# Later weight sums and an exchanged product in the up projection of a decoder trunk's MLP

## The chip, the cores and the metric

The kernel runs on one core of a Trainium2 chip. The metric is device time in microseconds (us) of one execution. TensorE (PE) multiplies, VectorE (DVE) and ScalarE (ACT) do elementwise work, GpSimd (POOL) is nearly unused in the part that changes, and SyncE (SP) issues most DMAs.

## The reference

A trunk of two layers works on x of 1024 x 1024 float32. Each layer is attention and then an MLP with a squared ReLU; the change touches the MLP alone.

```
def squared_relu_mlp(h, w_up, w_down):
    a = jax.nn.relu(h @ w_up)
    return (a * a) @ w_down

# in each layer i:
x = x + squared_relu_mlp(rmsnorm(x, mlp_norm_g[i]), mlp_w_up[i], mlp_w_down[i])
```

h is 1024 x 1024, w_up 1024 x 4096, w_down 4096 x 1024.

## The kernel before

**Products.** Both MLP matmuls are done by Strassen's scheme with seven products in place of eight (numbered 1 to 7, Winograd's form). Each product is itself done in three passes, since every operand is split into a high part (a copy in a rounded format, made by ACT, L99) and a low part (source less high part, made by DVE, L100): high by high, high by low, low by high, in lines L1700 to L1702.

**Up units.** `mlp` runs over 16 units (`NP`), each 256 columns of `w_up`. A unit has seven products of 12 matmuls of 128x512. Its weights come as two halves of 512 KB (`load_raw`, L1619), into two tiles `mr` for even units and two tiles `d` for odd ones. `gain_w` multiplies them by the norm's gain, eight ACT instructions (L1592). `sum_w` forms four weight sums on DVE (L1635 to L1638). `prep_w` splits one operand of a product (L99, L100) into one of seven pairs of tiles that go round; the loop asks for it three products ahead.

**Banks.** Products 1, 6, 7 and 4 of a unit add up in one PSUM bank (`psu`), 2 in a second, 5 and 3 in a third (`psv`). After 1, 6 and 5 ACT copies the bank out (L1743). After 2, 7 and 3 DVE adds bank and copy (L1756) and squares (L1735). After 4 ACT takes the ReLU (L1747) and DVE multiplies (L1748). So with the order 1, 2, 6, 5, 7, 3, 4 there is always a product in another bank between two that share one. Results go to DRAM (`hd`, L1738).

**Down.** `Down` reads them back and multiplies with `w_down`. Its `begin` is called after each product of the last unit: after product 6 it takes the tile `f0`, which held the X operand of product 6 (`mqf` in the trace), and issues four loads of `w_down` into it (`load_b`, L1859); after product 5 the same with `f1`. The first down steps split these loads and the results of the up units, and multiply into `psy` (L2053 to L2055).

**Order.** The code records instructions; a planner lays out each engine's queue from that. It starts what its own reckoning of time has ready and prefers what was recorded earlier among that. Each engine then runs its queue in that order. For units 0 and 1, whose products go 1, 2 early and then 6, 6, 5, 5, 7, 7, 3, 3, 4, 4, the order is written out by hand; `tc.issue_after` holds some of that work behind a given instruction.

Of the kernel before, what the change touches and what calls it, by code (L numbers as in the profile page):

```python
# [55 lines left out]
def trunk(  # L56
# [39 lines left out]
    def split(src, hi, lo, scale=None):  # L96

        if scale is None:
            r = nc.scalar.activation(hi, src, AF.Copy)  # L99
            return r, nc.vector.tensor_tensor(lo, src, f32(hi), ALU.subtract)  # L100
        else:
            nc.scalar.activation(hi, src, AF.Copy, scale=scale)
            nc.vector.scalar_tensor_tensor(lo, src, scale, f32(hi), ALU.mult, ALU.subtract)
# [845 lines left out]
    def units_of(h):  # L949
        return units if h < H - 1 else units_end  # L950
# [153 lines left out]
    seq = [(h, u) for h in range(H) for u in units_of(h)]  # L1104
# [78 lines left out]
    NP = FF // 256  # L1183
    TORD = list(range(NT))
    SUB = ALU.subtract

    def k4(ap):
        return ap.rearrange("p (k c) -> p k c", k=4)
# [419 lines left out]
    def mlp(layer, m, early_w=None, early_mm=None):  # L1608

        X, xr = m.X, m.xr  # L1610
        V, G = nc.vector, nc.vector.tensor_tensor
# [3 lines left out]
        def load_raw(i):  # L1615
            r = [m.raw() for _ in range(2)] if i % 2 == 0 else [m.t(f"d{j}") for j in range(2)]
            raws[i] = r = [t_.rearrange("p a (b c) -> p (a b) c", c=256) for t_ in r]
            for h in range(2):
                nc.sync.dma_start(out=r[h], in_=wsrc[:, 4 * h : 4 * h + 4, 256 * i : 256 * i + 256])  # L1619

        ss = []

        def gain_w(i):
            for h in range(2):
                scale_w(layer, raws[i][h], 4 * h)

        def sum_w(i):
            if i < 2:
                ss.append([m.t(f"i{j}")[:, 0, :] for j in (1, 3, 5)] if i == 0 else [*[m.t("d2")] * 2, m.t("i7")[:, 0, :]])
                if i == 1:  # L1630
                    ss[1][0:2] = [ss[1][0][:, j, :] for j in range(2)]
            r = raws.pop(i)
            a11, a12, a21, a22 = r[0][:, :, 0:P], r[1][:, :, 0:P], r[0][:, :, P:256], r[1][:, :, P:256]
            s1, s2, s4 = [k4(a) for a in ss[i % 2]]
            G(s1, a21, a22, ALU.add)  # L1635
            G(s2, s1, a11, SUB)
            G(a21, a11, a21, SUB)
            G(s4, a12, s2, SUB)  # L1638
            sums[i] = {1: a11, 2: a12, 3: s4, 4: a22, 5: s1, 6: s2, 7: a21}

        def pair(t_):
# [21 lines left out]
        def prep_w(i, p):  # L1663
            a = sums[i][p]
            n = hct[0]
            hct[0] += 1
            if n < 7:
                hl.append([k4(v) for v in opens[n]()])
            hi, lo = hl[n % 7]
            split(a, hi, lo)  # L1670
            return hi, lo
# [6 lines left out]
        def prep_x(p, cols=range(4)):  # L1678
            for j in cols:
                c = slice(j * P, (j + 1) * P)  # L1680
                if layer and (p != 6 and j < 2 or len(cols) == 4):
                    if j % 2:
                        continue
                    c = slice(j * P, (j + 2) * P)
                src = m.t2[j] if p == 6 else xr[{5: 0, 7: 1, 4: 2, 3: 3}[p]][:, :, c]
                hi, lo = [v[:, :, c] for v in X[p]]
                split(src, hi, lo)
# [83 lines left out]
                write(7, i, h)  # L1771

        seq = [(i, p) for p in (6, 5, 7, 3, 4) for i in range(2)]
        seq += [(i, p) for i in range(2, NP) for p in (1, 2, 6, 5, 7, 3, 4)]
        LA = 4
        ready = {}

        def go(i, p, w):
            evac(i, p, up_mm(i, p, w))
# [12 lines left out]
        else:  # L1792
            gain_w(0)
        sum_w(0)
        prep_x(6, range(3))
        load_raw(1)
# [5 lines left out]
        with tc.issue_after(m.last_n.ins):  # L1802
            gain_w(1)
        sum_w(1)
        ready[(1, 6)] = prep_w(1, 6)
        prep_x(5, (3,))
        ready[(0, 5)] = prep_w(0, 5)
        X[7] = [m.t("g0", F32R), m.t("g1", F32R)]
        X[3] = [m.t("g2", F32R), m.t("g3", F32R)]
        with tc.issue_after(m.last_n.ins):  # L1810
# [8 lines left out]
        for n, (i, p) in enumerate(seq):  # L1819
            for q_ in seq[n : n + LA]:  # L1820
                if q_ not in ready:
                    ready[q_] = prep_w(*q_)
            if (i, p) == (1, 7):
                load_raw(2)
                gain_w(2)
                sum_w(2)
            if p == 4 and 0 < i < NP - 2:
                load_raw(i + 2)
            if p == 2 and i < NP - 1:
                gain_w(i + 1)  # L1830
            if p == 6 and 2 <= i < NP - 1:
                sum_w(i + 1)
            go(i, p, ready.pop((i, p)))
            if i == NP - 1:
                dn.begin(p)
# [341 lines left out]

    jw, early = {}, []
    mlp(0, m0, lambda: jw.update(early_w()), early_mm)
    m0.rp.release()  # L2180
    kv1p = pool("kv1p")
# [183 lines left out]
    m1 = Mlp(1, x1)  # L2365
    wo_strassen(1, wq, [f0, f1], m1)
    mlp(1, m1)
    m1.rp.release()
    m1.s.release()
# [35 lines left out]
```

## Time and profile before

| what | value |
|---|---|
| median of 3 runs | 2110.15 us (2108.54 to 2110.25) |
| the profiled execution | 2112.17 us |
| its span, first to last instruction | 2110.5 us |
| PE busy | 2071.6 us (98%), 9880 matmuls |
| DVE, ACT busy | 1493.9 us (71%), 1142.9 us (54%) |
| up units of layer 0 and of layer 1 in the trace | about 541 to 854 and 1477 to 1797 us |

The profiled execution is one run of its own, 2.0 us above the median; 1.7 us of it lie outside the span. Matmuls are pipelined: one of 128x512 is shown with 0.39 us, and the next starts after about 0.23 us. A wait of PE is therefore seen best in the distance between two starts.

### The profile page before, as it was taken

To read this page: it belongs to the slowest core of one execution; us is meant where nothing else is said; L and a number is where in the kernel's file an instruction comes from. 1 tells how busy PE (TensorE), PEld (TensorE's weight loads), DVE (VectorE), ACT (ScalarE), POOL (GpSimd) and SP (SyncE) were. 2 spreads that over 40 slices of the span, in tenths; PEclk is the share of its full clock that TensorE was granted. 3 is DMA by queue.
4 is the path that set the end of the run, shared out by engine and by line. 5 is a ranking of instruction groups with operands and counts; after the bars stand their busy time and mean duration, and the time that the engine had idled before them with its cause. 6 is when DMAs were issued, how large, how long until landed. Compare 5 with 4: busy or idle time off the path is not lost.

```text
span 2110.5 us, 29217 instructions
## 1 busy us (share of the span) xinstructions
PE 2071.6 (98%) x9880; PEld 1699.8 (81%) x9880; DVE 1493.9 (71%) x2876; ACT 1142.9 (54%) x2461; POOL 204.7 (10%) x288
## 2 busy tenths in 40 slices
PE   7999999999999999999999999999999999999998
PEld 6988778778778888788888878778788887888887
DVE  7555688865977766797667543897976775976565
ACT  5445477776744453444445553877845443444452
POOL 0013100000000000031111231631000000000000
PEclk9999999999999999999999999999999999999999
DMA  7202123343254445976653211146344446844332
GB/s 247 68 1 76 46 63 90 105 146 100 96 184 146 139 154 195 325 254 205 212 165 95 75 31 30 41 156 234 122 152 146 165 140 225 316 152 154 117 119 90
DMA packets 181632, 294.47 MB, mean 140 GB/s; under 512 B 18557, under 2 KB 74346, under 8 KB 181482
## 3 DMA queue, kind: packets, MB, share of 16 engines
q1 hardware_dynamic: 171008, 264.25, 38.9%
q0 software_dynamic: 8048, 25.70, 3.5%
q10 hardware_dynamic: 2426, 2.65, 0.4%
q8 instruction: 78, 1.28, 0.2%
q14 instruction: 72, 0.59, 0.1%
HBM read 194.81 MB, written 85.25 MB: 133 GB/s over the span
## 4 chain that ended last, share of the span: by engine, by line
PE 76%; DVE 8%; DMA 8%; ACT 5%; issue 2%; SPq 0%; POOL 0%; DVEq 0%; ACTq 0%; POOLq 0%
PE psy L2053 5%; PE psy L2055 5%; PE psy L2054 5%; PE psz L2054 4%; PE psz L2053 4%; PE psz L2055 4%; PE pss L964 4%; PE pso L1006 3%; PE psu L1700 3%; PE psu L1702 3%; PE psu L1701 3%; DMA mr<-in_mlp_w_up_dram 3%; DMA d<-in_mlp_w_up_dram 3%; PE psf L108 2%; PE psf L110 2%; PE psf L109 2%
## 5 line engine op out<-in xcount | busy, mean ns | idle before, releaser
L1592 ACT ACTIVATE mr<-mr,gcol 128x256 f32<-128x256 f32 (+1 forms) x160 | 67.7, 479 | 79.0 <-DMA mr<-in_mlp_w_up_dram 64.4
L2053 PE MATMUL psy<-g 128*128 128x512 f32 x256 | 99.9, 390 | 0.0
L2054 PE MATMUL psy<-g 128*128 128x512 f32 x256 | 99.6, 389 | 0.0
L2055 PE MATMUL psy<-g 128*128 128x512 f32 x256 | 99.3, 389 | 0.0
L1592 ACT ACTIVATE d<-d,gcol 128x256 f32<-128x256 f32 x128 | 57.3, 499 | 75.5 <-DMA d<-in_mlp_w_up_dram 65.4
L99 ACT ACTIVATE g<-i 128x512 fp32r<-128x512 f32 x79 | 49.6, 628 | 88.3 <-PE psz L2054 41.2
L99 ACT ACTIVATE i<-mr 128x512 fp32r<-128x512 f32 x86 | 54.0, 628 | 68.6 <-PE psz L2054 20.0
L985 ACT ACTIVATE p<-pss 128x512 f32<-128x512 f32 x108 | 63.6, 593 | 41.1 <-PE pss L964 41.0
L100 DVE TENSOR_TENSOR g<-i,g 128x512 fp32r<-128x512 f32 x79 | 55.6, 704 | 40.7 <-ACT g L99 40.6
L99 ACT ACTIVATE uh<-i 128x512 fp32r<-128x512 f32 x66 | 41.6, 630 | 76.9 <-PE psy L2054 35.7
L100 DVE TENSOR_TENSOR pl<-p,ph 128x512 fp32r<-128x512 f32 (+1 forms) x96 | 61.6, 651 | 27.6 <-ACT ph L99 27.1
L839 DVE TENSOR_REDUCE m<-psx 128x1 f32<-128x128 f32 (+5 forms) x96 | 70.2, 748 | 11.0 <-PE psx L835 10.8
L2053 PE MATMUL psz<-g 128*128 128x512 f32 x192 | 74.7, 389 | 0.0
L2054 PE MATMUL psz<-g 128*128 128x512 f32 x192 | 74.7, 389 | 0.0
L2055 PE MATMUL psz<-g 128*128 128x512 f32 x192 | 74.7, 389 | 0.0
L100 DVE TENSOR_TENSOR uh<-i,uh 128x512 fp32r<-128x512 f32 x66 | 45.5, 689 | 36.7 <-ACT uh L99 36.7
L100 DVE TENSOR_TENSOR i<-mr,i 128x512 fp32r<-128x512 f32 x78 | 53.6, 687 | 21.2 <-ACT i L99 21.0
L99 ACT ACTIVATE ph<-p 128x512 fp32r<-128x512 f32 (+1 forms) x96 | 56.4, 599 | 1.3
L1928 DVE TENSOR_TENSOR mqf<-mqq,mqf 128x512 f32<-128x512 f32 x64 | 43.0, 687 | 19.3 <-DMA mqq<-in_mlp_w_down_dram 19.2
L2055 PEld LDWEIGHTS psy<-g 128*128 128x128 f32 x256 | 48.0, 188 | 10.0
L2053 PEld LDWEIGHTS psy<-g 128*128 128x128 f32 x256 | 48.1, 188 | 9.9
L2054 PEld LDWEIGHTS psy<-g 128*128 128x128 f32 x256 | 48.1, 188 | 9.8
(746 smaller groups left out, 6972.8 us busy)
## 6 DMA issues: line engine op xcount, KB each, us to landing
i<-hd SPq DMA_DIRECT2D x154, 256.0 KB
hd<-uh SPq DMA_DIRECT2D x76, 256.0 KB
hd<-ul SPq DMA_DIRECT2D x76, 256.0 KB
mr<-in_mlp_w_up_dram SPq DMA_DIRECT2D x36, 512.0 KB
hd<-x SPq DMA_DIRECT2D x72, 256.0 KB
mr<-hd SPq DMA_DIRECT2D x70, 256.0 KB
d<-in_mlp_w_up_dram SPq DMA_DIRECT2D x32, 512.0 KB
mqq<-in_mlp_w_down_dram SPq DMA_DIRECT2D x32, 512.0 KB
```

What stands on the lines that cost most here:

```text
L99: r = nc.scalar.activation(hi, src, AF.Copy)
L100: return r, nc.vector.tensor_tensor(lo, src, f32(hi), ALU.subtract)
L839: nc.vector.reduce_max(m8s[h][:, i : i + 1], ps[:, c], axis=AX, negate=True)
L964: return lambda: nc.tensor.matmul(o, a, b, skip_group_check=True, **kw)
L985: nc.scalar.activation(p, ps, AF.Exp, scale=SC)
L1006: mms.append(lambda: nc.tensor.matmul(o, a, b, skip_group_check=True, **kw))
L1592: nc.scalar.activation(w[:, k, :], w[:, k, :], AF.Copy, scale=g_mlp[layer][:, k0 + k : k0 + k + 1])
L1700: nc.tensor.matmul(ps, wh[:, k, :], xh[:, k, :], start=p in (1, 2, 5) and k == 0, stop=False, skip_group_check=True)
L1701: nc.tensor.matmul(ps, wh[:, k, :], xl[:, k, :], start=False, stop=False, skip_group_check=True)
L2053: nc.tensor.matmul(ps, ah[:, j, :], bh, start=p in (1, 5, 2) and k == 0, stop=False, skip_group_check=True)
L2054: nc.tensor.matmul(ps, ah[:, j, :], bl, start=False, stop=False, skip_group_check=True)
L2055: nc.tensor.matmul(ps, al[:, j, :], bh, start=False, stop=k == NP - 1, skip_group_check=True)
```

## The change

Three edits, in both layers. (1) Of the four sums of unit 0, the last two (`a21` and `s4`, L1637 and L1638) are recorded after the operand splits for (1, 6) and (0, 5) and the last columns of the X operands of 6 and 5. (2) In the last unit, product 6 comes second: 1, 6, 2, 5, 7, 3, 4. Operand splits and `begin(6)` follow that order. (3) For units 3 to 15, `gain_w` is recorded ahead of the previous unit's product 6 (before: of its product 2), and `sum_w` ahead of its product 5 (before: of its product 6).

```
-        ss = []
+        ss, held = [], []
...
             G(s1, a21, a22, ALU.add)
             G(s2, s1, a11, SUB)
-            G(a21, a11, a21, SUB)
-            G(s4, a12, s2, SUB)
+
+            def rest():
+                G(a21, a11, a21, SUB)
+                G(s4, a12, s2, SUB)
+
+            if i:
+                rest()
+            else:
+                held.append(rest)
...
-        seq += [(i, p) for i in range(2, NP) for p in (1, 2, 6, 5, 7, 3, 4)]
+        seq += [(i, p) for i in range(2, NP) for p in ((1, 2, 6, 5, 7, 3, 4) if i < NP - 1 else (1, 6, 2, 5, 7, 3, 4))]
...
         ready[(0, 5)] = prep_w(0, 5)
+        held[0]()
...
-            if p == 2 and i < NP - 1:
+            if p == 6 and 2 <= i < NP - 1:
                 gain_w(i + 1)
-            if p == 6 and 2 <= i < NP - 1:
+            if p == 5 and 2 <= i < NP - 1:
                 sum_w(i + 1)
```

## Rows read from the trace of the kernel before

**Rows 1.** The page: busy time and share of each engine.
```profile
PE 2071.6 (98%) x9880; PEld 1699.8 (81%) x9880; DVE 1493.9 (71%) x2876; ACT 1142.9 (54%) x2461; POOL 204.7 (10%) x288
```
**Rows 2.** Waits of PE: us in total, times, longest us.
```profile
PE psu L1700 <- ACT d L1743: 3.3, 7, 1.4
```
**Rows 3.** Timeline of PE, layer 0, end of up: start, us, instruction, [idle before].
```profile
850.82 0.39 PE L1702 MATMUL psv<-g,d 128*128 128x512 f32 x1
851.35 0.50 PE L1700 MATMUL psu<-x,d 128*128 128x512 f32 x1
851.70 0.40 PE L1701 MATMUL psu<-x,d 128*128 128x512 f32 x1
...
857.20 0.39 PE L2054 MATMUL psy<-g 128*128 128x512 f32 x1
858.57 0.50 PE L2053 MATMUL psy<-i,i 128*128 128x512 f32 x1 [0.99 <-DVE ul L1748]
```
**Rows 4.** Timeline of PE, layer 1, the same place.
```profile
1793.11 0.39 PE L1702 MATMUL psv<-g,d 128*128 128x512 f32 x1
1793.82 0.50 PE L1700 MATMUL psu<-x,d 128*128 128x512 f32 x1 [0.31 <-DVE x L1756]
...
1799.61 0.39 PE L2054 MATMUL psy<-g 128*128 128x512 f32 x1
1801.03 0.50 PE L2053 MATMUL psy<-i,i 128*128 128x512 f32 x1 [1.03 <-DVE ul L1748]
```
**Rows 5.** Timeline of DVE, layer 0, end of up.
```profile
850.00 0.69 DVE L100 TENSOR_TENSOR i<-mqf,i 128x512 fp32r<-128x512 f32 x1 [8.22 <-ACT i L99]
850.61 0.69 DVE L1756 TENSOR_TENSOR x<-psu,i 128x512 f32<-128x512 f32 x1
...
857.83 0.68 DVE L1748 TENSOR_TENSOR ul<-psu,ul 128x512 f32<-128x512 f32 x1
```
**Rows 6.** Timeline of ACT, layer 0, end of up.
```profile
837.96 0.58 ACT L1743 ACTIVATE d<-psu 128x512 f32<-128x512 f32 x1
...
849.34 0.63 ACT L99 ACTIVATE i<-mqf 128x512 fp32r<-128x512 f32 x1 [2.87 <-DMA mqf<-in_mlp_w_down_dram]
```
**Rows 7.** Timeline of SP's queue, layer 0, end of up.
```profile
843.08 5.82 SPq L1859 DMA_DIRECT2D mqf<-in_mlp_w_down_dram  x8
```
**Rows 8.** Timeline of PE, layer 0, products 1 and 2 of the last unit.
```profile
837.22 0.39 PE L1702 MATMUL psu<-mqq,i 128*128 128x512 f32 x1
837.45 0.39 PE L1700 MATMUL psv<-mqq,i 128*128 128x512 f32 x1
```
**Rows 9.** Timeline of ACT in a middle unit of layer 0.
```profile
708.63 0.91 ACT L1592 ACTIVATE mr<-mr,gcol 128x256 f32<-128x256 f32 x2 [3.09 <-DMA mr<-in_mlp_w_up_dram]
...
709.96 0.57 ACT L1743 ACTIVATE d<-psu 128x512 f32<-128x512 f32 x1
```
**Rows 10.** Timeline of PE, product 7 of the same unit.
```profile
710.59 0.50 PE L1700 MATMUL psu<-g,i 128*128 128x512 f32 x1
```
**Rows 11.** Timeline of DVE, layer 1, start of up.
```profile
1489.83 0.68 DVE L1637 TENSOR_TENSOR mr<-mr 128x512 f32<-128x512 f32 x1
...
1492.84 0.69 DVE L1532 TENSOR_TENSOR i<-x,x 128x512 f32<-128x512 f32 x1
```
**Rows 12.** Timeline of ACT, the same place.
```profile
1493.91 0.62 ACT L99 ACTIVATE mqf<-i 128x512 fp32r<-128x512 f32 x1
```
**Rows 13.** Timeline of PE, the same place: the first product of 6.
```profile
1494.59 0.49 PE L1700 MATMUL psu<-mqf,i 128*128 128x512 f32 x1 [1.31 <-ACT mqf L99]
```
**Rows 14.** Windows, start and end of up: engines in page order, PEclk, DMA, GB/s.
```profile
1494.40:1499.40 5.00, 4.51 (x12) 3.35 (x13) 5.00 (x9) 5.00 (x10) 0.00 (x0) 0.66 0.00 0
854.00:860.00 6.00, 5.01 (x22) 3.84 (x21) 6.00 (x11) 0.60 (x1) 0.00 (x0) 1.00 1.04 390
```
**Rows 15.** Timeline of DVE, layer 0, ahead of the up units.
```profile
533.26 0.68 DVE L1638 TENSOR_TENSOR i<-mr,i 128x512 f32<-128x512 f32 x1
```
**Rows 16.** Timeline of PE, the same place.
```profile
540.07 1.09 PE L1320 MATMUL psT_m<-ident,d 128*128 128x128 f32 x8 [0.21 <-ACT d L1309]
```

## The prediction

> **What bounds the kernel now.** I read the page first. PE is busy for 2071.6 us, 98% of the span [rows 1], so no edit here can win more than a wait of PE that it removes; nothing else counts unless it makes one. Then the waits of PE. Its largest wait in the MLPs is for the copy of a bank by ACT, 3.3 us in seven waits [rows 2]. Then the timelines, engine by engine, around each place where the edits work. A regular matmul starts 0.23 us after the one before [rows 8], so what exceeds that in a distance of two starts is lost, waits too short for the waits view included.
>
> At the end of layer 0's up units PE loses time twice. Product 4 starts 0.53 us after the last matmul of product 3, 0.30 too late, and its second matmul follows after 0.35, another 0.12 that a restart costs. The first down step stands still from 857.20 to 858.57, 1.14 too long, with a restart again [rows 3]. Together 0.30 + 1.14 + 2 x 0.12 = 1.68 us. In layer 1 the two distances are 0.71 and 1.42 us, 0.48 and 1.19 too long [rows 4], and with two restarts the sum is 1.91. The releaser in both is DVE, and DVE shows why: it sat idle for 8.22 us until 850.00, waiting for the split of the first `w_down` load, with the bank of product 7 queued behind that split though product 7 had made its last matmul at 850.82 - 2.72 = 848.10 and was done by 848.5; from there to 858.51 it works without a pause up to the product-4 result that PE needs [rows 5]. ACT began that split at 849.34, when the load landed [rows 6]; the load was issued at 843.08, when product 6 had let go of `f0` [rows 7].
>
> **The exchanged product.** What it takes: product 6 must wait until ACT has copied product 1 out of the same bank. Product 1's last matmul starts at 837.22 [rows 8] and the copy runs from 837.96 to 838.54 [rows 6]; a matmul starts 0.06 after such a copy ends (709.96 + 0.57 = 710.53, then 710.59) [rows 9, 10]. So 6 can start at 838.60 and not at 837.45: a hole of 1.15 us, room for five matmuls. Product 2 is ready and writes another bank. If it fills the hole, the cost is near nothing (0 to one matmul and a restart, 0.35); if PE's queue holds 6 strictly ahead, it is 1.15 + 0.12 = 1.27. I take filled, 0.15 a layer, because the queues here follow readiness: at 857.20 PE ran a matmul of a later down step (operands in `g`) ahead of one of step 0 (operands in `i`) that waited for its bank [rows 3]. Behind the waiting matmul stand the rest of 2 and all of 5, whose results nobody needs for another product.
>
> What it gives: a product is 12 x 0.227 = 2.72 us, so 6 ended at 837.45 + 2 x 2.72 = 842.89 and now ends at 838.60 + 2.72 = 841.32, filled or not. The four loads into `f0` start 1.57 us earlier. In SP's queue they now pass the write of product 2's result (256 KB) and whatever waits for product 2's X operand; these come 1.15 to 2.7 us later, and none is read before the down steps are well under way. With the same 6.26 us from issue to use (849.34 - 843.08), ACT splits at 847.8 and DVE at 848.4. Product 7's bank is then taken when it is ready, about 848.5 to 849.0, and not at 850.61. The 7.90 us from there to the end of the product-4 result (858.51) end at about 856.9. PE, without the first wait, needs it at 857.43 - 0.42 = 857.01. Both waits go; what is late next is the same result, 0.1 us before PE, so I keep 0.1 a layer. Gain 1.68 + 1.91 = 3.59, less 0.2, less 0.3 for the holes: 3.1 us. Bounds: 3.6 if nothing is left of either; no gain if the loads land no earlier because others fill the DMA engines.
>
> **The held sums.** Two DVE instructions of 0.68 us move behind others in the same layer. In layer 1 they ran at 1489.83 and after, ahead of the X work that ends in L1532 at 1492.84 [rows 11], which ACT splits at 1493.91 [rows 12], for which PE waited 1.31 us [rows 13]. In the 5.0 us after that PE had 0.66 of its clock [rows 14]. At most the wait goes and the 12 matmuls run in 2.7 us and not in about 5: 1.3 + 2.3 = 3.6. I take nothing. In that stretch DVE waits for ACT's copies between the X steps and takes whatever is ready; if the sums leave, the splits recorded after them come first, and the sums, ready, fill the same gaps later. And ACT did not start its split when L1532 ended (1493.53) but 0.4 later. In layer 0, L1638 ran early, at 533.26 [rows 15], in the busy stretch before a transpose that waited 0.21 [rows 16]; moved behind it, up to 0.4 with the restart comes back. I take 0.2. A loss: the sums are read first by the splits for products 7 and 3 of unit 0, which come after 6, 6, 5, 5, and DVE has the same sum of work before these; nothing is priced.
>
> **Scalings and sums a product later.** Nothing is added. The pair of scalings at 708.63 [rows 9] stands before product 7 at 710.59 [rows 10]. Product 4 of that unit comes 2 x 2.72 later, at 716.0; product 4 of unit 15 is at 851.35 [rows 3], 135.3 us or 7.1 units of 7 x 2.72 on. So it is unit 8, and `mr` holds even units: these are unit 10's scalings, recorded in unit 9. They run a unit ahead of their place because they start when their load lands (3.09 us waited for it), so moving the place by one product changes nothing that is ready at that time. I cost it at nothing; what hides it is that lead. If it did decide the order, it would cost or give what the next part says.
>
> **Sum.** -3.59 + 0.2 + 0.3 - 0.2 = -3.3 us. The profiled execution took 2112.17, so 2108.9 in its terms; it lies 2.02 above the median, 2110.15, so the median goes to 2106.8. About 0.2%, 4.2 us, is what a measurement of this kernel can tell from no change, that is 2105.9 to 2114.4.
>
> **Rivals.**
>
> *The start of layer 1 gains.* If the held sums really leave DVE's path there, 1 to 3.5 us of the 3.6 come on top: 2103.3 to 2105.8. For it: PE waits for exactly this chain [rows 13]. Against: the gaps that the sums can fill.
>
> *The copy comes out ahead of the scalings.* Product 6's copy at 709.96 stood behind the pair of scalings that waited for its load [rows 9], and product 7 began as the copy ended. With the order turned round in every unit, the 3.3 us [rows 2] and some short waits come back, about 4 us: 2103.
>
> *More scalings before the copy (the other side).* The same edit could put both pairs there instead of one: 0.9 us more [rows 9] in each of some 24 units, as the copy has no slack now. 24 x 0.9 = 21 us less 3.3: about 2128. It outweighs the gain from the fourth unit on.
>
> *The hole stays empty.* 2 x 1.27 in place of 0.3: -1.1 us, 2109.1.
>
> *The loads land no earlier.* Some microseconds later the DMA engines are full, a share of 1.04 at 390 GB/s [rows 14]. If the six microseconds of these loads are spent behind other transfers, an earlier issue only waits longer. Then 0.3 and -0.2 are left, 2110.2, and with empty holes 2112.5. Against: what stands ahead of them in SP's queue gets less. The Trainium skill, "DMA: Bandwidth & Descriptors", section "Anatomy of one DMA", gives about 2 us plus bytes over 436 GB/s for a DMA (fitted on the other issue path), an estimate of 3.2 us for 512 KB. The trace has 6.3, so by the page half of it is queueing, which is what this rival needs; it would cost the sum 3.4 us.
>
> *The clock falls in the hole.* After the 1.31 us wait PE ran at 0.66 on average, that is partly at the lower of its two levels [rows 13, 14], though not after the wait of 0.99, in whose window it was 1.00 [rows 3, 14]. At half clock 12 matmuls take 2.7 us more: 2 x (2.7 + 1.27) - 3.4 = +4.5, 2114.7. The Trainium skill, "TensorE: Matmul & The Clock Gate", section "A second HAM failure mode: psum-queue depth-cycling", tells of short idling between groups on PSUM banks that lowers the clock; here a wait of 0.99 us shows none of it, one of 1.31 does.
>
> **How the numbers follow.** Forecast 0.33; start of layer 1 0.20; copy first 0.15; empty hole 0.09; loads no earlier 0.10; clock 0.03; more scalings 0.10. Faster by over 0.2%: the second and third, 0.35. Within 0.2%: forecast, empty hole and late loads, 0.52. Slower: 0.13. The range 2101.5 to 2112.5 holds all but the clock, the further scalings and what the third may give beyond its price. The forecast's own range is 2105.9 to 2108.5.
>
> **What would show it.** In the profile after: five or so matmuls of product 2 between 1 and 6 of unit 15; the first `mqf` load some 1.6 us earlier against product 1, its split likewise; no wait of PE for L1756 or L1748 at the end of up; product 7 of the middle units waiting as before, and each unit's scalings in the same place of ACT's queue; PE's 1.31 us at the start of layer 1 still there. Wrong would be a split of `mqf` that starts no earlier, a hole of 1.2 us without matmuls, or other waits in the middle units.

## The result and the profile after

| what | before | after |
|---|---|---|
| median, same chip | 2109.36 us (20 runs, 2107.11 to 2116.12) | 2113.32 us (20 runs, 2107.11 to 2118.67) |
| ratio after to before | | 1.0018, 95% interval 1.001 to 1.0025 |
| the profiled execution, its span | 2112.17, 2110.5 us | 2117.15, 2115.4 us |

By the ratio, the change makes the kernel 3.8 us slower (2.1 to 5.3; 0.0018 of 2109.36), where 3.3 us faster was forecast; the time lies outside the range that was stated. In the kernel after, lines up to L1636 keep their numbers, those behind move by 2 to 8: L1700 to L1702 are now L1707 to L1709, L1743 is L1750, L1756 is L1763, L1748 is L1755, L1637 and L1638 are L1639 and L1640, L1859 is L1867, L2053 is L2061.

The page's line of busy times, kernel after; PE's busy time is up by only 0.7 us on [rows 1], where the span grew by 4.9, so most of the loss is waiting:

```profile
PE 2072.3 (98%) x9880; PEld 1698.8 (80%) x9880; DVE 1494.7 (71%) x2876; ACT 1142.1 (54%) x2461; POOL 204.5 (10%) x288
```

**The end of the up units** went as forecast. Timeline of PE after, layer 0, end of product 1 to start of product 6, then end of product 3, and the first down step (against [rows 3, 8]):

```profile
837.57 0.39 PE L1709 MATMUL psu<-mqq,i 128*128 128x512 f32 x1
837.79 0.39 PE L1707 MATMUL psv<-mqq,x 128*128 128x512 f32 x1
...
838.70 0.39 PE L1708 MATMUL psv<-mqq,x 128*128 128x512 f32 x1
838.94 0.50 PE L1707 MATMUL psu<-mqf,i 128*128 128x512 f32 x1
...
851.33 0.39 PE L1709 MATMUL psv<-g,d 128*128 128x512 f32 x1
851.55 0.39 PE L1707 MATMUL psu<-x,d 128*128 128x512 f32 x1
...
854.04 0.39 PE L1709 MATMUL psu<-x,d 128*128 128x512 f32 x1
854.27 0.39 PE L2061 MATMUL psy<-i,i 128*128 128x512 f32 x1
```

Five matmuls of product 2 fill the hole, product 6 starts 1.37 us after the last matmul of product 1 (forecast 1.38), and neither product 4 nor the first down step waits. The chain behind it, from the timelines of SP, ACT and DVE after (against [rows 5 to 7]):

```profile
842.00 1.92 SPq L1867 DMA_DIRECT2D mqf<-in_mlp_w_down_dram  x4
```

```profile
846.69 0.63 ACT L99 ACTIVATE i<-mqf 128x512 fp32r<-128x512 f32 x1 [4.03 <-DMA mqf<-in_mlp_w_down_dram]
```

```profile
849.09 0.69 DVE L1763 TENSOR_TENSOR x<-psu,i 128x512 f32<-128x512 f32 x1 [1.04 <-PE psu L1709]
```

The load is issued 4.43 us after the last matmul of product 1, where it was 5.86, and the add of product 7's bank (L1763) now waits for PE, no longer for the split. From issue to use the load took 4.69 us here, not the 6.26 that the prediction kept, so the split gains as much from a shorter load as from the earlier issue.

**The middle units** went as forecast too: the pair of scalings stands where it stood in ACT's queue, ahead of product 6's copy (after; against [rows 9]):

```profile
708.95 0.91 ACT L1592 ACTIVATE mr<-mr,gcol 128x256 f32<-128x256 f32 x2 [2.86 <-DMA mr<-in_mlp_w_up_dram]
...
710.28 0.58 ACT L1750 ACTIVATE d<-psu 128x512 f32<-128x512 f32 x1
```

**The start of layer 1's units** is where the time went. Timeline of PE after: the instructions that wait, around units 0 to 2, and the stretch behind them. Before, no distance of two starts from 1505 to 1545 exceeds 0.24:

```profile
1494.79 0.49 PE L1707 MATMUL psu<-mqf,i 128*128 128x512 f32 x1 [1.32 <-ACT mqf L99]
...
1511.07 0.50 PE L1707 MATMUL psu<-g,x 128*128 128x512 f32 x1 [0.70 <-ACT x L99]
...
1523.64 0.39 PE L1709 MATMUL psu<-x,d 128*128 128x512 f32 x1
1524.99 0.50 PE L1707 MATMUL psv<-mqq,i 128*128 128x512 f32 x1 [0.96 <-ACT i L99]
...
1526.51 0.50 PE L1707 MATMUL psv<-mqf,x 128*128 128x512 f32 x1 [0.79 <-ACT x L99]
...
1529.26 0.79 PE L1709 MATMUL psv<-mqq,i 128*128 128x512 f32 x1 [2.01 <-DVE i L100]
1529.85 0.63 PE L1707 MATMUL psv<-mqq,i 128*128 128x512 f32 x1
...
1534.97 0.42 PE L1708 MATMUL psu<-mqq,i 128*128 128x512 f32 x1
```

```profile
1523.91 0.39 PE L1702 MATMUL psu<-x,d 128*128 128x512 f32 x1
1524.14 0.39 PE L1700 MATMUL psu<-mqq,i 128*128 128x512 f32 x1
```

The second fence is before: product 1 of unit 2 follows unit 1's last matmul in 0.23 us. After, its weights are not there; PE takes two matmuls of product 2 (from 1524.99), then two of product 5, waits 2.01 us, and the twelve distances from 1529.85 to 1534.97 are 0.43 us each, half clock. The windows view of that stretch after gives the granted clock as 0.50 (PEclk, the third number from the end):

```profile
1529.26:1534.97 5.71, 5.71 (x14) 4.45 (x15) 5.35 (x9) 0.93 (x3) 0.00 (x0) 0.50 0.78 281
```

What exceeds 0.227 in the distances from 1505 to 1545 sums up to 8.4 us after and 0.0 before.

What is late is unit 2's weights. Timelines of DVE, before and then after:

```profile
1508.68 0.69 DVE L100 TENSOR_TENSOR i<-i,i 128x512 fp32r<-128x512 f32 x1
1509.28 0.69 DVE L100 TENSOR_TENSOR d<-mr,d 128x512 fp32r<-128x512 f32 x1
...
1515.74 0.69 DVE L1635 TENSOR_TENSOR i<-mr,mr 128x512 f32<-128x512 f32 x1 [1.13 <-ACT mr L1592]
```

```profile
1508.89 0.68 DVE L100 TENSOR_TENSOR i<-i,i 128x512 fp32r<-128x512 f32 x1
1509.50 0.68 DVE L1763 TENSOR_TENSOR ul<-psu,d 128x512 f32<-128x512 f32 x1
1511.05 0.69 DVE L100 TENSOR_TENSOR x<-d,x 128x512 fp32r<-128x512 f32 x1 [0.87 <-ACT x L99]
1511.66 0.69 DVE L100 TENSOR_TENSOR x<-i,x 128x512 fp32r<-128x512 f32 x1
1512.26 0.68 DVE L100 TENSOR_TENSOR d<-mr,d 128x512 fp32r<-128x512 f32 x1
...
1522.37 0.69 DVE L1635 TENSOR_TENSOR i<-mr,mr 128x512 f32<-128x512 f32 x1 [3.05 <-ACT mr L1592]
```

The split `d<-mr` is that of (0, 4), the last reader of the second `mr` half of unit 0. Up to the instruction before it DVE is 0.21 us behind, as PE is; the split itself is 2.98 behind, because an add and two splits now stand ahead of it. The load that it releases, in SP's timeline before and after:

```profile
1504.25 6.13 SPq L1619 DMA_DIRECT2D mr<-in_mlp_w_up_dram  x2
1511.05 0.37 SPq L1619 DMA_DIRECT2D d<-in_mlp_w_up_dram  x1
```

```profile
1504.46 0.38 SPq L1619 DMA_DIRECT2D mr<-in_mlp_w_up_dram  x1
1511.77 0.38 SPq L1619 DMA_DIRECT2D d<-in_mlp_w_up_dram  x1
...
1513.56 0.39 SPq L1619 DMA_DIRECT2D mr<-in_mlp_w_up_dram  x1
```

Before, both `mr` halves go out ahead of unit 3's (`d`), the second at about 1504.25 + 6.13 - 0.38 = 1510.0; after, it comes 1.8 us behind one of unit 3's, and the other follows it within 0.5. Its scalings on ACT, before and after:

```profile
1514.00 1.71 ACT L1592 ACTIVATE mr<-mr,gcol 128x256 f32<-128x256 f32 x4 [0.44 <-DMA mr<-in_mlp_w_up_dram]
```

```profile
1520.62 1.71 ACT L1592 ACTIVATE mr<-mr,gcol 128x256 f32<-128x256 f32 x4 [2.59 <-DMA mr<-in_mlp_w_up_dram]
```

They begin 6.6 us later: the issue is 3.6 later, and from issue to use it takes 7.1 us and not 4.0.

### The profile page after: what moved, and what is told of

It is laid out like the page before. It is cut to its first block, busy times and chain, and to the rows that moved or that the text cites. A ratio compares the mean times of both kernels' runs of the same rounds, so it can differ in the third digit from the quotient of the medians.

```text
span 2115.4 us, 29217 instructions
## 1 busy us (share of the span) xinstructions
PE 2072.3 (98%) x9880; PEld 1698.8 (80%) x9880; DVE 1494.7 (71%) x2876; ACT 1142.1 (54%) x2461; POOL 204.5 (10%) x288
## 4 chain that ended last, share of the span: by engine, by line
PE 81%; DVE 8%; DMA 5%; ACT 4%; issue 2%; POOL 0%; SPq 0%; DVEq 0%; ACTq 0%
PE psy L2061 5%; PE psy L2063 5%; PE psy L2062 5%; PE psz L2063 4%; PE psz L2062 4%; PE psz L2061 4%; PE psu L1707 4%; PE pss L964 4%; PE psu L1709 4%; PE psu L1708 4%; PE pso L1006 3%; PE psv L1709 2%; PE psv L1707 2%; PE psv L1708 2%; PE psf L108 2%; PE psf L110 2%
## 5 line engine op out<-in xcount | busy, mean ns | idle before, releaser
L2061 PE MATMUL psy<-g 128*128 128x512 f32 x256 | 99.9, 390 | 0.0
L2061 PE MATMUL psz<-g 128*128 128x512 f32 x192 | 74.7, 389 | 0.0
L2061 PEld LDWEIGHTS psy<-g 128*128 128x128 f32 x256 | 48.1, 188 | 9.9
```

Source lines behind the costliest of these rows:

```text
L2061: nc.tensor.matmul(ps, ah[:, j, :], bh, start=p in (1, 5, 2) and k == 0, stop=False, skip_group_check=True)
```

## Experiments

Each is compared with the kernel before on the same chip. Theory A: the exchange gains what it should, the held sums lose it and more in layer 1, the later scalings do nothing. The other theories are named where a run tests them. "Excess" below is the sum of what exceeds 0.227 us in PE's distances of starts, over the distances above 0.26.

**The three edits apart.** The exchange alone:

```
+        seq += [(i, p) for i in range(2, NP) for p in ((1, 2, 6, 5, 7, 3, 4) if i < NP - 1 else (1, 6, 2, 5, 7, 3, 4))]
```

> The kernel before with edit 2 alone: in the last unit the products go 1, 6, 2, 5, 7, 3, 4. Theory A (the held sums cost what was lost, the exchange keeps its gain): 3 to 3.5 us faster than before, about -0.16%; five matmuls of product 2 between 1 and 6 of unit 15, no wait of PE for L1756 or L1748 at the end of up in either layer, and the start of layer 1's up units as before (one wait of 1.3 us, product 1 of unit 2 on time). Theory B (the exchange makes the loss by moving transfers): slower by 3 us or more.

Measured: 2107.7 us against 2110.39, ratio 0.9991 (0.9982 to 1.0).

The held sums alone:

```
...
+            if i:
+                rest()
+            else:
+                held.append(rest)
...
+        held[0]()
```

> The kernel before with edit 1 alone: the last two sums of unit 0 recorded later, in both layers. Theory A: slower by 6 to 8 us (+0.3 to +0.4%), all of it in layer 1 between product 7 of unit 1 and product 1 of unit 2, with waits of PE for the splits of unit 2 (about 1, 1 and 2 us) and some ten matmuls at the lower clock; the second half of unit 2's weights lands 5 us or more later than before against the first product 6. Theory C (the later scalings and sums of edit 3 make the loss): no change.

Measured: 2116.16 us, ratio 1.003 (1.0018 to 1.0041). The trace has the same four waits as the full change and a half clock behind them, an excess of 7.1 us from 1505 to 1545.

The scalings and sums a product later, alone:

```
-            if p == 2 and i < NP - 1:
+            if p == 6 and 2 <= i < NP - 1:
                 gain_w(i + 1)
-            if p == 6 and 2 <= i < NP - 1:
+            if p == 5 and 2 <= i < NP - 1:
                 sum_w(i + 1)
```

> The kernel before with edit 3 alone: scalings and sums of units 3 to 15 recorded one product later. Theory A: no change, within 1 us (0.05%), the order of ACT's and DVE's queues differing in units 2 to 4 only and PE's waits for product 7 of the middle units as before. Theory C: slower by 4 us or more, with the late splits at unit 2 of layer 1.

Measured: 2109.57 us, ratio 0.9995 (0.9986 to 1.0004). In its trace the queues of ACT and DVE differ from those before only at 588 to 615 and 1521 to 1529 us, in units 2 and 3. Exchange and later scalings without the held sums:

```
-        seq += [(i, p) for i in range(2, NP) for p in (1, 2, 6, 5, 7, 3, 4)]
+        seq += [(i, p) for i in range(2, NP) for p in ((1, 2, 6, 5, 7, 3, 4) if i < NP - 1 else (1, 6, 2, 5, 7, 3, 4))]
...
-            if p == 2 and i < NP - 1:
+            if p == 6 and 2 <= i < NP - 1:
                 gain_w(i + 1)
-            if p == 6 and 2 <= i < NP - 1:
+            if p == 5 and 2 <= i < NP - 1:
                 sum_w(i + 1)
```

> The changed kernel without edit 1, that is edits 2 and 3. Theory A: 3 to 3.5 us faster than before, as the exchange alone. Theory C: slower than before.

Measured: 2109.87 us, ratio 1.0002 (0.9993 to 1.0011). The loss belongs to the held sums: 0.0030 of 2110 is 6.3 us. The exchange's gain is smaller than 3.1 us, though: 0.0009 of 2110 is 1.9 (0 to 3.8), and in the fourth run nothing of it is left. That run's trace does have the gain where it belongs: PE loses 0.2 us at the end of up in each layer, and 0.5 from 1505 to 1545. Against the trace of the exchange alone it loses 1.4 us more in the first 300 us and 1.8 more from 1300 to 1477, where no edit works. Such scatter is as large as the gain; whether the two edits together also cost something is not shown.

**Which link of the chain.** The full change, with the split for (0, 4) of layer 1 ahead of others in DVE's queue:

```
                 if q_ not in ready:
-                    ready[q_] = prep_w(*q_)
+                    with tc.high_priority(offset=20) if layer and q_ == (0, 4) else __import__("contextlib").nullcontext(): ready[q_] = prep_w(*q_)
```

> The full change, but in layer 1 the operand split for (0, 4) is recorded with a higher priority, so that DVE makes its low part ahead of three other instructions and the second half of the weights of unit 2 can be loaded about 3 us earlier. Theory A (the loss is the late load): the four waits of PE at the start of unit 2 in layer 1 go, with the half-clock stretch behind them, some 7 of 8 us; 2106 to 2108 us. Rival B (the held sums cost by taking DVE later, whatever is loaded when): the waits stay, 2113. Rival C (the loss comes from layer 0's part): 2113 too.

Measured: 2107.09 us against 2110.66, ratio 0.9983 (0.9974 to 0.9992). The full change with unit 3's loads behind unit 2's in SP's queue, where PE's order is the same as after, DVE's differs in one pair of instructions, and ACT's in the scalings of unit 3 and some splits of unit 2:

```
-                nc.sync.dma_start(out=r[h], in_=wsrc[:, 4 * h : 4 * h + 4, 256 * i : 256 * i + 256])
+                lastload[i] = nc.sync.dma_start(out=r[h], in_=wsrc[:, 4 * h : 4 * h + 4, 256 * i : 256 * i + 256])
...
-                load_raw(i + 2)
+                with tc.issue_after(lastload[2].ins) if layer and i == 1 else __import__("contextlib").nullcontext(): load_raw(i + 2)
```

> The full change, but in layer 1 the loads of unit 3 are queued behind the second half of unit 2's. The split for (0, 4) stays late, so this half is still issued some 2.5 us later than before, but no longer shares the DMA engines with a load ahead of it. Theory A with the order on DVE as the main part: the waits shrink by less than half, about 2111 us. Theory A with the DMA queue as the main part (7.0 us from issue to use after, 4.0 before): the waits mostly go, about 2108. Rival B: no change, 2113.

Measured: 2108.41 us, ratio 0.9994 (0.9984 to 1.0004). PE's waits from 1500 to 1540 (us in total, times, longest) after, with the early split, and with the loads in order:

```profile
PE psv L1709 <- DVE i L100: 2.0, 1, 2.0
PE psv L1707 <- ACT i L99: 1.0, 1, 1.0
PE psv L1707 <- ACT x L99: 0.8, 1, 0.8
PE psu L1707 <- ACT x L99: 0.7, 1, 0.7
```

```profile
PE psu L1707 <- ACT x L99: 1.1, 1, 1.1
```

```profile
PE psv L1709 <- DVE i L100: 1.6, 1, 1.6
```

With the early split all three waits at the start of unit 2 and the half clock are gone, and 0.0035 of 2110, 7.4 us, are back: theory A, and rivals B (DVE is taken later, whatever is loaded when) and C (layer 0) fall. The planner also moved some splits and sums after it, so it is the order around this split that is shown, not one instruction to the nanosecond. With only the loads in order the split still comes late; its timeline of ACT:

```profile
1514.32 1.71 ACT L1592 ACTIVATE mr<-mr,gcol 128x256 f32<-128x256 f32 x4 [0.83 <-DMA mr<-in_mlp_w_up_dram]
```

The second half was issued at about 1509.9 (1500.94 + 9.37 - 0.4 from SP's queue) and used 4.4 us later, not 7.1. Against the full change the ratio falls by 0.0024, 5 us. In the trace the excess from 1505 to 1545 falls from 8.4 to 1.8 us, but part of that is luck: this execution lost 1.6 us more right behind its wait of 1.3 us, at half clock, which gave the load that much more time. Counted over 55 us from 2 us ahead of the end of that wait, the excess is 10.6 after, 9.3 with the held sums alone, 8.5 in the repeat below, 5.6 with the loads in order, 3.7 with the early split, and 3.5 to 3.8 in the six traces that don't hold the sums in layer 1. So the larger part of the loss hangs on the order of the loads. Not all of it need be the load itself: ACT's first split of unit 2 behind the scalings came 2.1 us after their start, where it was 3.7 after, since the planner moved it as well. Nor does the run separate the load of unit 3 that had got ahead from the one that followed within 0.5 us; both went behind.

The Trainium skill, "DMA: Bandwidth & Descriptors", section "Anatomy of one DMA", gives 2 us plus bytes over 436 GB/s for a DMA (fitted on another issue path), an estimate of 3.2 us for one such load. The 4.0 and 4.4 us from issue to use here lie 0.8 and 1.2 above it; the 7.1 were measured with loads of the same size close ahead and behind.

The full change with the sums held in layer 0 only:

```
-            if i:
+            if i or layer:
                 rest()
...
-        held[0]()
+        for f_ in held: f_()
```

> The full change, but the two sums are held in layer 0 only; in layer 1 they are recorded where they were. Theory A: no loss at the start of layer 1's units, the same as the change without the held sums, 2109 to 2110 us. Rival C (holding them in layer 0 costs as well): 2111 or more.

Measured: 2107.88 us, ratio 0.9986 (0.9977 to 0.9995). Holding them in layer 0 costs nothing that can be measured (forecast: a gain of 0.2). From here to the full change it is 1.0018 - 0.9986, 6.8 us, for layer 1 alone. Taken from the change without the held sums (1.0002) it would be 3.4; the two starting points differ by the scatter named above.

**A version that is faster, and two repeats.** On top of the early split, unit 2's scalings behind two splits in layer 1:

```
-                gain_w(2)
+                with tc.issue_after(lastload[(1, 7)].ins) if layer else __import__("contextlib").nullcontext(): gain_w(2)
...
-            split(a, hi, lo)
+            lastload[(i, p)] = split(a, hi, lo)[0]
```

> The version with the early split for (0, 4), and in layer 1 also the scalings of unit 2's first half queued on ACT behind the two splits for (1, 7). In the run before this one these splits stood behind four such scalings, and PE waited 1.1 us for them. If that order is the cause, the wait goes and the time falls by about 1.2 us, to 2105.5 to 2106.5; unless the four scalings, now 1 us later, hold up the sums of unit 2 in turn, then no change.

Measured: 2107.79 us against 2111.33, ratio 0.9985 (0.9974 to 0.9996). Timeline of ACT:

```profile
1506.69 0.63 ACT L99 ACTIVATE x<-d 128x512 fp32r<-128x512 f32 x1 [1.17 <-DVE x L100]
1507.23 0.61 ACT L99 ACTIVATE x<-i 128x512 fp32r<-128x512 f32 x1
1507.75 1.69 ACT L1592 ACTIVATE mr<-mr,gcol 128x256 f32<-128x256 f32 x4
```

The order is as meant and the wait of 1.1 us is gone; the excess from 1505 to 1545 falls from 1.5 to 0.3. The time that was expected for it, 2105.5 to 2106.5, did not come, and the ratio does not show a gain: 1.2 us is 0.0006, less than either interval's half width. Both versions beat the kernel before, by 3.6 and 3.2 us.

> The full change as it is, on the same chip as the version above. Theory A: the waits at the start of unit 2 in layer 1 come from the order of the queues and stand there again, 7 to 9 us with the half-clock stretch; 2112 to 2114. If they were an accident of one execution they are gone or much smaller, and the time is nearer 2108.

The full change once more measured 2113.93 us, ratio 1.0015 (1.0006 to 1.0025). PE's waits from 1500 to 1540:

```profile
PE psv L1709 <- DVE i L100: 2.0, 1, 2.0
PE psv L1707 <- ACT x L99: 0.8, 1, 0.8
PE psv L1707 <- ACT i L99: 0.6, 1, 0.6
PE psu L1707 <- ACT x L99: 0.4, 1, 0.4
```

The same four waits, the half clock again, 6.4 us of excess: they belong to the order, not to one execution.

> The kernel before, for one more profile. In the first one the load that the end of the up units waits for took 6.3 and 6.4 us from issue to use, and PE lost 1.7 and 1.9 us there; in the two runs without the exchange the load took 4.9 to 5.4 us and PE lost 0.4 to 0.9. If this varies from one execution to the next, the profile here lies somewhere between 0.8 and 3.6 us for both layers together; if the later scalings or the held sums did it, it is 3.6 again.

The kernel before once more measured 2110.53 us in one run. Timeline of ACT, the splits at the end of up in layer 0 and layer 1:

```profile
847.93 0.63 ACT L99 ACTIVATE i<-mqf 128x512 fp32r<-128x512 f32 x1 [2.01 <-DMA mqf<-in_mlp_w_down_dram]
...
1790.10 0.63 ACT L99 ACTIVATE i<-mqf 128x512 fp32r<-128x512 f32 x1 [3.15 <-DMA mqf<-in_mlp_w_down_dram]
```

Their loads were issued at 842.53 and 1783.56, so they took 5.4 and 6.5 us; PE lost 0.9 and 2.0 us. The four traces without the exchange lost 3.6, 2.9 (both the kernel before), 1.6 (later scalings alone) and 1.2 (held sums alone) in the two layers together, 2.3 on average, with 4.9 to 6.5 us from issue to use, 5.7 on average. The eight traces with the exchange lost 0.3 to 0.7, with 4.3 to 5.6 us, 4.7 on average. So the same program differs from one execution to the next in layer 0 (1.7 and 0.9 us), but in layer 1 both lost 1.9 to 2.0; that the smaller losses of the other two are chance, and not their edits, is not shown.

## Why the prediction was wrong, point by point

**The exchange.** The mechanism was right at each link but one: the hole is filled, the loads go out 1.4 us earlier (forecast 1.6), the bank of product 7 is taken when it is ready, both waits are gone. Not forecast was that the loads also take less time from issue to use, 4.7 us on average and not 5.7; the prediction kept 6.26. "The hole stays empty", "the loads land no earlier" and "the clock falls in the hole" did not happen. The size may have been off: the 3.59 us were those of one execution, the most that any of the four traces without the exchange lost. By the mean of the four, 2.3, the gain is 2.3 - 0.4 = 1.9 us where 3.1 stood in the sum; by the two of the kernel before alone it is 2.8. The exchange alone measured 1.9 (0 to 3.8), which does not decide between them.

**Later scalings and sums.** Nothing was forecast and nothing was resolved: 0.9995 (0.9986 to 1.0004), and the queues of the middle units did not change. Neither "the copy comes out ahead of the scalings" nor "more scalings before the copy" shows in the traces.

**The held sums, the step that failed.** The prediction took nothing in layer 1, and of a loss it said: "DVE has the same sum of work before these; nothing is priced." The first half was right. The splits came first, and the sums later; timeline of DVE after:

```profile
1493.05 0.68 DVE L1532 TENSOR_TENSOR i<-x,x 128x512 f32<-128x512 f32 x1
...
1499.07 0.68 DVE L1639 TENSOR_TENSOR mr<-mr 128x512 f32<-128x512 f32 x1
```

L1532 started no earlier (1493.05 against 1492.84, PE being 0.20 later too), the wait of 1.3 us stayed, and by 1508.89 DVE had done the same work with the same delay as PE. So "the start of layer 1 gains" fell because the splits took the sums' place. The gaps that the prediction also named are not there: DVE is busy for 5.00 of 5.00 us in [rows 14]. But equal work is not equal order. The prediction followed the sums to their readers and stopped there; it didn't ask which instruction gives back the buffer that the next load needs. Behind 1508.9 the new order put the split for (0, 4) last of four, 3 us later; that let a load of another unit pass on SP's queue, which made 3 us into 6.4; and unit 2 started with waits of 0.96, 0.79 and 2.01 us and twelve matmuls at half clock. Price: 6.1 to 6.8 us by three pairs of ratios (held alone; the full change twice, each against held in layer 0 only), 2.7 and 3.4 if the full change is set against the run without the held sums. The traces put it between: over the 55 us counted above, the three with this order lose 9.5 us on average and the six that don't hold the sums in layer 1 lose 3.6, so 5.8. The 8.4 and 6.4 us behind 1505 are more than that, since the held sums also remove 1.1 us ahead of it: a wait of 0.7 to 0.8 us with its restart near 1500, which the other orders have where the clock stays up.

Sum with these sizes: -1.9 for the exchange, +5.8 to +6.5 for the held sums, 0 for the scalings: +3.9 to +4.6 us; measured +3.8 (2.1 to 5.3). The chance of 0.13 that the prediction gave to a slower kernel stood on two other rivals, and neither of them happened. What makes the planner turn the order round at 1508.9 was not tried.

## What to carry to other kernels

When work is recorded later, follow not only who reads its result but which buffers its neighbours give back, and which load is waiting for each; here a split that slipped by 3 us cost about 6, and much of that came from another load that took its place in the queue. Equal work up to a point in an engine's queue says nothing about the order behind it: if an order is computed and not written, ask for each buffer's last reader whether something can pass it. And a wait that ends with a DMA varies from one execution to the next, so a gain read from a single profile should carry that spread: here two executions of one program lost 2.9 and 3.6 us at the same place, 0.9 and 1.7 of it in layer 0.

## What the runs showed of the hardware

The half clock of [rows 14] was not a property of the kernel. The same program, profiled again, waits 1.32 us for the same instruction and keeps its clock. Windows view of that second execution of the kernel before, 5 us from about the end of the wait (PEclk is the third number from the end):

```profile
1493.55:1498.55 5.00, 3.74 (x15) 2.57 (x15) 5.00 (x9) 5.00 (x10) 0.00 (x0) 1.00 0.00 0
```

All twelve traces (the two shown first and ten of the experiments) have this wait, 1.31 to 1.33 us; three were partly at half clock afterwards (a granted clock of 0.66 over the 5 us behind it, as in [rows 14]) and nine not (1.00). After the three waits of unit 2, the last of them 2.0 us, all three traces that have them were (after, 0.50 in the stretch shown above). The step from 1.3 us of wait to a slow stretch is thus a matter of chance here, and its price belongs in the range of a forecast, not in a term. That price was small where the sums are not held: over the 14 us from 2 us ahead of the wait's end, the two traces with a slow stretch lost 3.8 us and the four without one 3.2, because those four wait 0.7 us again some 5 us later. With the sums held, it is 3.8 against 2.2.
